# Layer 1's modulation vectors as row sums on VectorE, during layer 0's feed-forward block

## Chip, core and metric

One Trainium2 chip, one of its cores, one launch of the whole program. The metric is the time of the launch on the device in microseconds (us). The trace is that of one profiled execution; the times shown are of separate runs.

## What is computed

A two-layer trunk over 512 latent tokens and 256 context tokens with a model width of 1024. Each layer first makes six modulation vectors of 1024 values per stream (latent: from `c`; context: from `c_ctx`), then runs a mixer and a SwiGLU feed-forward block, each behind a modulated RMS norm. Cut to what matters here:

```python
silu_c, silu_cc = jax.nn.silu(c), jax.nn.silu(c_ctx)
for l in range(DEPTH):                                  # 2 layers
    m  = silu_c  @ ada_w[l] + ada_b[l]                  # (1024) @ (1024, 6144)
    mc = silu_cc @ ada_w[l] + ada_b[l]
    sh_m, sc_m, g_m, sh_f, sc_f, g_f = split(m, 6)
    csh_m, csc_m, cg_m, csh_f, csc_f, cg_f = split(mc, 6)
    h, hc = rms_norm(x) * (1 + sc_m) + sh_m, rms_norm(ctx) * (1 + csc_m) + csh_m
    ...                                                 # layer 0: diff. attention and DeltaNet; layer 1: neighbourhood attention
    x = x + g_m * o
    x = x + g_f * swiglu(rms_norm(x, norm_ffn[l]) * (1 + sc_f) + sh_f)
    if l == 0:                                          # the context is dropped after layer 0
        ctx = ctx + cg_m * oc
        ctx = ctx + cg_f * swiglu(rms_norm(ctx) * (1 + csc_f) + csh_f)
return x
```

In layer 1 the context uses its modulation only for the shift and scale ahead of the mixer (`csh_m`, `csc_m`); its other four vectors are not used.

## The kernel before

Activations lie transposed: eight tiles of 128 model channels by 768 token columns (256 of the context, 512 latent). Every large product is done as three float32r matmuls on high and low parts (`mm3`, L176): the weight tile is loaded into a staging tile `st` by SyncE's DMA queue (SP), its high part `whi` is a copy on ScalarE (L164), its low part `wlo` is a subtraction on VectorE (L165).

Layer 0's feed-forward block (`ffn`) runs in four groups of hidden tiles (6, 5, 6 and 5). An *up step* is one hidden tile: two weight tiles of 128x1024 (gate and up), then for each stretch of tokens two rows of 24 matmuls into PSUM tiles `f`, Silu on ScalarE, the product `sg` on VectorE (L1409), and its parts `mh` (ScalarE, L1410) and `ml` (VectorE, L1411). A *down tile* is one of eight column tiles of the group's down projection: one weight tile, two rows of matmuls (512 latent, 256 context columns), and the update of `x` on VectorE (L1421).

The *entrance* of the block is where the mixer's output projection and the block's norm overlap. The tokens go in thirds (context, then each half of the latent tokens). For each third eight updates `x<-o` (L1332) run on VectorE, squares on ScalarE (L294) and their sums on VectorE or GpSimd (L296). `finish` (L298 on) then makes the mean `ms` (L309), the inverse root (a seed `rs_y` on VectorE, L190, then a chain of small steps on GpSimd, L193 to L202), its broadcast `rb` on TensorE (L313), and for each of eight channel tiles the normed tile `nt` (L316) and its parts `hhi` (ScalarE, L324) and `hlo` (VectorE, L325; the last tile's on GpSimd). The first hidden tile's up step takes the three thirds one by one, as they come.

Layer 1's modulation vectors are made while layer 0's feed-forward block runs. `ada_gen` is a generator with one step for each of 48 tiles of `ada_w` (128x1024, 512 KB): a DMA into the staging tile `ast` (two buffers, SP's queue, L1380) and four matmuls with 32 stationary columns into the PSUM tile `adacc` (L238). After each eighth tile the sums are copied to `adrow` (L243), turned by two transposes (`adtp`, L249) and added to the bias (L252). `ada_step` asks for one step: ahead of each weight split of an up step (two per hidden tile), and ahead of the one split of a down tile. 48 steps thus lie in group 0 (6 hidden tiles, 8 column tiles), group 1 (5 and 8) and five hidden tiles of group 2. A scheduler then sets the order on each engine from the program's dependencies and priorities; engines run their instructions in that order.

```python
for t in range(t0, t0 + ng):
    ws = []
    for z in range(2):
        ada_step()
        ws.append(kx.wsplit(a["wfi"][l, t, z], 1024))
    for s, sl in (segs if t else fine):
        up(mh, ml, ws, sl)
...
for c in range(KT - tail):
    ada_step()
    ws = kx.wsplit(a[f"wfo{gi}"][l, c], 128 * ng)
    for s, sl in segs:
        down(mids, c, ws, s, sl, cnt)
```

Of the kernel before, what the change touches and what calls it, by code (L numbers as in the profile page):

```python
# [15 lines left out]
D = 1024  # L16
# [3 lines left out]
KT = 8  # L20
# [51 lines left out]
def MARK(name):  # L72
    pass
# [51 lines left out]
def build(tc, a, out, dbg=None):  # L125
    nc = tc.nc
    V, G, S, T, DMA = nc.vector, nc.gpsimd, nc.scalar, nc.tensor, nc.sync
    es = ExitStack()
    with es:
# [4 lines left out]
        def ct(name, shape, dt=F32):  # L134
            return cp.tile(shape, dt, name=name, tag=name)
# [10 lines left out]
        def load_const(name, key, shape):  # L146
            t = ct(name, shape)
            DMA.dma_start(out=t, in_=a[key])
            return t

        cvec = load_const("cvec", "cT", [128, KT, 2])
        ada_b = load_const("ada_b", "ada_b", [128, 2, 48])
        nrm = load_const("nrm", "nrm", [128, 2, 2, KT])

        def wstage(src, n):
            st = wp.tile([128, n], F32, name="st", tag="st", bufs=2)
            if src is not None:
                DMA.dma_start(out=st, in_=src)
            return st

        def wsplit(src, n, tiles=None):
            st = wstage(src, n)
            hi, lo = tiles or [wp.tile([128, n], F32R, name="w" + t, tag="w" + t, bufs=3) for t in ("hi", "lo")]
            S.activation(out=hi, in_=st, func=AF.Copy)  # L164
            V.tensor_tensor(out=lo, in0=st, in1=hi.bitcast(F32), op=ALU.subtract)  # L165
            return hi, lo

        nops = []
        dep = mybir.DependencyInfo(mybir.DependencyClass.Sync, mybir.DependencyReason.DATA)

# [14 lines left out]
        def rsqrt(pool, v, n, tag="rs", N=None):  # L185
            N = N or V
            y = pool.tile([128, n], F32, name="rs_y", tag=tag + "y")
            t = pool.tile([128, n], F32, name="rs_t", tag=tag + "t")
            vh = pool.tile([128, n], F32, name="rs_v", tag=tag + "v")
            V.tensor_scalar(  # L190
                out=y.bitcast(I32), in0=v.bitcast(I32), scalar1=1, scalar2=-1, op0=ALU.logical_shift_right, op1=ALU.bitwise_xor
            )
            N.tensor_scalar(out=y, in0=y, scalar1=RS_SEED, scalar2=None, op0=ALU.mult)  # L193
            N.tensor_scalar(out=vh, in0=v, scalar1=-0.5, scalar2=None, op0=ALU.mult)
            for _ in range(3):
                N.tensor_tensor(out=t, in0=y, in1=y, op=ALU.mult)
# [25 lines left out]
        scal = {}  # L222

        def ada_block(*args, **kw):
            for _ in ada_gen(*args, **kw):
                pass

        def ada_gen(l, b, psp, mk, stage=None, gap=1200, kg=KT):
            lab(f"ada{l}{b}")
            sc = ct(f"scal{l}{b}", [128, 2, 16])  # L230
            for hf in range(2):
                row = cp.tile([128, 256], F32, name="adrow", tag="adrow")
                for k in range(KT):
                    st = (stage or wstage)(a["ada_w"][l, b, hf, k], 1024)
                    if k % kg == 0:
                        acc = psp.tile([128, 256], F32, name="adacc", tag=mk)
                    for j in range(4):
                        T.matmul(  # L238
                            out=acc[32 * j:32 * j + 32, :], lhsT=scT[:, k, :], rhs=st[:, 256 * j:256 * j + 256],
                            start=(k % kg == 0), stop=(k % kg == kg - 1), tile_position=(0, 32 * j),  # L240
                        )
                    if k == kg - 1:
                        V.tensor_copy(out=row, in_=acc)  # L243
                    elif k % kg == kg - 1:
                        V.tensor_tensor(out=row, in0=acc, in1=row, op=ALU.add)
                    yield 450, gap
                tp = psp.tile([128, 2, 128], F32, name="adtp", tag=mk)
                for q in range(2):
                    T.transpose(out=tp[:, q, :], in_=row[:, q * 128:q * 128 + 128], identity=ident)  # L249
                for s in range(2):  # L250
                    o = 16 * b + 8 * hf
                    V.tensor_tensor(  # L252
                        out=sc[:, s, 8 * hf:8 * hf + 8].rearrange("p (j q) -> p j q", q=2),
                        in0=tp.rearrange("p q (j u) -> p j q u", u=32)[:, :, :, s],
                        in1=ada_b[:, l, o:o + 8].rearrange("p (j q) -> p j q", q=2), op=ALU.add,
                    )
            names = [("sh_m", "sc_m"), ("g_m", "sh_f"), ("sc_f", "g_f")][b]
            for i, nm in enumerate(names):
                for s in range(2):
                    v = sc[:, s, 8 * i:8 * i + 8]  # L260
                    if nm.startswith("sc"):
                        w = 0 if nm == "sc_m" else 1
                        t = ct(f"gain{l}{w}{s}", [128, KT])
                        V.scalar_tensor_tensor(out=t, in0=v, scalar=1.0, in1=nrm[:, l, w, :], op0=ALU.add, op1=ALU.mult)
                        scal[l, "a_m" if w == 0 else "a_f", s] = t
                    else:
                        scal[l, nm, s] = v
            yield 500, 0

        def new_h(lat_only=False):  # L270
            hi = [hp.tile([128, NT], F32R, name=f"hhi{k}", tag=f"hhi{k}") for k in range(KT)]
            lo = [hp.tile([128, NT], F32R, name=f"hlo{k}", tag=f"hlo{k}") for k in range(KT)]
            return hi, lo

        class Norm:
            def __init__(self, x, l, w, pool, ps, segs):
                self.on_v, self.rs, self.lo_g = NORMS[f"n{l}{w}"]
                self.x, self.pool, self.ps, self.segs = x, pool, ps, segs
                self.av = [scal[l, "a_" + w, s] for s in range(2)]
                self.sv = [scal[l, "sh_" + w, s] for s in range(2)]  # L280
                self.ssq = [None] * len(segs)
                self.h = None

# [49 lines left out]
        kx = types.SimpleNamespace(**env)  # L333
# [9 lines left out]
        hi, lo = new_h()  # L343
# [18 lines left out]
        with tc.tile_pool(name="x0", bufs=1) as x0p:  # L362
# [13 lines left out]
            for j in range(4):  # L376
# [15 lines left out]
                r = rsqrt(x0p, ms, 6)  # L392
                rb = x0p.tile([128, NT], F32, name="rb", tag="rb")
                for i, sl in enumerate((CTX, LAT)):
                    n = sl.stop - sl.start
                    bp = x0v.tile([128, n], F32, name="bp", tag=f"v{4 + i}")
                    for j in range(n // 128):
                        c = sl.start // 128 + j
# [968 lines left out]
def ffn(kx, x, l, nm, next_norm):  # L1367
    tc, nc, a = kx.tc, kx.nc, kx.a
    V, G, S, T, DMA = nc.vector, nc.gpsimd, nc.scalar, nc.tensor, nc.sync
    scal, gs = kx.scal, kx.gs  # L1370
# [3 lines left out]
    hi, lo = nm.h  # L1374

    with tc.tile_pool(name="fp", bufs=2) as fp:
# [4 lines left out]
            return st  # L1381

        def adas():
            for b in range(3):
                yield from kx.ada_gen(1, b, gs, "C", stage=astage, kg=KT)

        ada_it = adas() if l == 0 else iter(())

        def ada_step():
# [260 lines left out]
def layout(inp):  # L1650
    import numpy as np

    g = {k: np.asarray(v) for k, v in inp.items()}
    f = np.ascontiguousarray
    o = {}
# [4 lines left out]
    cv = np.stack([g["c"][0], g["c_ctx"]], axis=-1)  # L1660
    o["cT"] = f(cv.reshape(KT, 128, 2).transpose(1, 0, 2))
    o["ada_w"] = f(g["ada_w"].reshape(2, KT, 128, 3, 2, 1024).transpose(0, 3, 4, 1, 2, 5))
    o["ada0"] = f(g["ada_w"][0, :, 0:2048].reshape(KT, 128, 2, 4, 2, 128).transpose(3, 1, 0, 2, 4, 5).reshape(4, 128, KT, 4, 128))
    o["ada_b"] = f(g["ada_b"].reshape(2, 48, 128).transpose(2, 0, 1))
    nr = np.stack([g["norm_mix"], g["norm_ffn"]], axis=1)
# [10 lines left out]
    w = g["even_w_in"][0]  # L1676
# [16 lines left out]
    w = g["odd_w_in"][0]  # L1693
# [54 lines left out]
```

## Time and profile before

| | |
|---|---|
| three runs | 1989.01, 1991.40, 1993.08 us (median 1991.4) |
| the profiled execution | 1988.47 us, span of the trace 1986.7 us |
| mean granted TensorE clock, share of full speed | 0.979 |
| busy in the span | TensorE 94%, VectorE 51%, ScalarE 37%, GpSimd 13% |
| HBM | 202.39 MB read, 32.99 MB written, mean 118 GB/s |
| DMAs of the 48 weight tiles concerned | 512 KB each, median 3.6 us from issue to landing |

Times in a row of the trace are microseconds from the span's start. A row of the timeline gives start, duration, engine, line, operation, result<-operands, shapes and count; what stands in brackets is the engine's idle time ahead of it and what ended that. The chain of waits is followed back from the end: a row there is a stretch of the span that this work sets. PE is TensorE, DVE VectorE, ACT ScalarE, POOL GpSimd, SP SyncE.

### The profile page before, as it was taken

How to read it: one execution, taken by the hardware profiler on the slowest of the kernel's cores; microseconds unless marked ns; L12 is line 12 of the kernel's file. 1: busy time of each engine (PE TensorE's matmuls, PEld its weight loads, DVE VectorE, ACT ScalarE, POOL GpSimd, SP SyncE). 2: the span in 40 equal slices, each digit the busy share in tenths (PEclk: the TensorE clock that was granted, in tenths of full speed). 3: DMA queues.
4: the chain of work that ended last, by engine and by line, in shares of the span. 5: the costliest groups of instructions: out<-in, count | busy, mean ns of one | idle time of the engine just before them, and what ended most of it. 6: DMA issues, size and time to landing. Idle time of an engine off the chain costs nothing.

```text
span 1986.7 us, 30896 instructions
## 1 busy us (share of the span) xinstructions
PE 1863.4 (94%) x12066; PEld 1629.6 (82%) x12066; DVE 1013.8 (51%) x2340; ACT 743.9 (37%) x1681; POOL 257.1 (13%) x360
## 2 busy tenths in 40 slices
PE   4978999798989999999999999989999989999999
PEld 3867889677868888888888888989999878888887
DVE  6566788776676662232222232456565663434333
ACT  3435454345664342112112112355555443223221
POOL 2132314421210130000000000321101020000000
PEclk8989999899999999999999999999999989999999
DMA  7556644547444623333343121211211213323232
GB/s 292 156 180 205 205 144 146 179 142 210 112 157 132 226 96 115 120 123 109 119 138 125 56 75 52 87 45 63 65 59 45 71 40 106 106 76 116 85 106 95
DMA packets 105074, 237.41 MB, mean 119 GB/s; under 512 B 10880, under 2 KB 48000, under 8 KB 103904
## 3 DMA queue, kind: packets, MB, share of 16 engines
q1 hardware_dynamic: 92400, 207.26, 32.5%
q0 software_dynamic: 4064, 14.38, 2.6%
q10 hardware_dynamic: 8464, 13.79, 2.0%
q8 instruction: 95, 1.56, 0.3%
q14 instruction: 51, 0.42, 0.1%
HBM read 202.39 MB, written 32.99 MB: 118 GB/s over the span
## 4 chain that ended last, share of the span: by engine, by line
PE 75%; DMA 9%; DVE 7%; ACT 4%; issue 3%; POOL 2%; SPq 0%; ACTq 0%; DVEq 0%; POOLq 0%
PE f L176 46%; PE d L176 15%; DMA qkd<-ar 3%; PE o L176 2%; PE adacc L238 2%; PE vp L448 1%; PE sc L1556 1%; PE o L1581 1%; DMA st<-in_ada_w_dram 1%; DVE cv L351 1%; PE m L854 1%; DMA qkvd<-cv 1%; PE S L1150 1%; PE m L1570 1%; PE t L1178 1%
## 5 line engine op out<-in xcount | busy, mean ns | idle before, releaser
L164 ACT ACTIVATE whi<-st 128x1024 fp32r<-128x1024 f32 (+4 forms) x219 | 212.2, 970 | 608.3 <-PE f L176 456.9
L176 PE MATMUL f<-hhi,whi 128*128 128x512 f32 (+1 forms) x1088 | 381.4, 353 | 3.2 <-ACT hhi L324 3.2
L176 PE MATMUL f<-hlo,whi 128*128 128x512 f32 (+1 forms) x1088 | 381.1, 351 | 0.6 <-DVE hlo L325 0.6
L176 PE MATMUL f<-hhi,wlo 128*128 128x512 f32 (+1 forms) x1088 | 380.2, 350 | 0.0
L165 DVE TENSOR_TENSOR wlo<-st,whi 128x1024 fp32r<-128x1024 f32 (+4 forms) x219 | 247.1, 1129 | 257.6 <-ACT whi L164 253.4
L176 PE MATMUL d<-whi,hhi 128*128 128x256 f32 (+1 forms) x800 | 235.2, 296 | 21.2 <-ACT ar L207 13.9
L176 PEld LDWEIGHTS f<-hhi,whi 128*128 128x128 f32 x1088 | 207.1, 191 | 36.1 <-ACT whi L164 5.4
L176 PE MATMUL d<-wlo,hhi 128*128 128x256 f32 (+1 forms) x800 | 232.9, 292 | 1.3 <-DVE wlo L165 1.3
L176 PE MATMUL d<-whi,hlo 128*128 128x256 f32 (+1 forms) x800 | 232.2, 292 | 0.0
L176 PEld LDWEIGHTS f<-hlo,whi 128*128 128x128 f32 x1088 | 207.6, 191 | 28.0 <-DVE hlo L325 1.2
L176 PEld LDWEIGHTS f<-hhi,wlo 128*128 128x128 f32 x1088 | 207.8, 191 | 26.8 <-issue 0.4
L176 PEld LDWEIGHTS d<-whi,hhi 128*128 128x128 f32 x800 | 156.9, 197 | 28.0 <-ACT ar L207 15.1
L176 PE MATMUL f<-mh,whi 128*128 128x512 f32 (+1 forms) x478 | 171.3, 360 | 0.0
L176 PE MATMUL f<-ml,whi 128*128 128x512 f32 (+1 forms) x478 | 170.0, 356 | 0.0
L176 PE MATMUL f<-mh,wlo 128*128 128x512 f32 (+1 forms) x478 | 168.9, 356 | 0.0
L176 PEld LDWEIGHTS d<-wlo,hhi 128*128 128x128 f32 x800 | 157.3, 197 | 2.5 <-DVE wlo L165 1.7
L176 PEld LDWEIGHTS d<-whi,hlo 128*128 128x128 f32 x800 | 156.6, 196 | 1.0
L1409 DVE TENSOR_TENSOR sg<-f,sg 128x512 f32<-128x512 f32 (+1 forms) x68 | 40.1, 589 | 229.5 <-PE f L176 228.8
L1421 DVE SCALAR_TENSOR_TENSOR x<-f,scal,x 128x256 f32<-128x256 f32 (+1 forms) x101 | 64.1, 639 | 169.0 <-PE f L176 168.7
L296 POOL TENSOR_TENSOR ssq<-ssq,sq 128x256 f32<-128x256 f32 x39 | 31.0, 797 | 677.4 <-ACT sq L294 676.2
L176 PE MATMUL d<-hhi,whi 128*128 128x512 f32 (+1 forms) x304 | 107.2, 353 | 5.0 <-ACT cin L207 2.6
L176 PEld LDWEIGHTS f<-mh,whi 128*128 128x128 f32 x478 | 90.2, 189 | 18.5 <-issue 6.2
(373 smaller groups left out, 3416.9 us busy)
## 6 DMA issues: line engine op xcount, KB each, us to landing
st<-in_wfi_dram SPq DMA_DIRECT2D x88, 512.0 KB, 3.5
ast<-in_ada_w_dram SPq DMA_DIRECT2D x48, 512.0 KB, 3.6
st<-in_ada_w_dram SPq DMA_DIRECT2D x32, 512.0 KB, 4.0
st<-in_wfo_dram SPq DMA_DIRECT2D x32, 384.0 KB, 3.0
st<-in_wfo_dram SPq DMA_DIRECT2D x32, 320.0 KB, 2.8
aw<-in_ada_dram SPq DMA_DIRECT2D x8, 1024.0 KB, 12.3
st<-in_w1kv_dram SPq DMA_DIRECT2D x16, 512.0 KB, 3.8
aqT<-qkd SPq DMA_DIRECT2D x48, 128.0 KB, 3.2
```

Of the source, the lines that this page charges most:

```text
L164: S.activation(out=hi, in_=st, func=AF.Copy)
L165: V.tensor_tensor(out=lo, in0=st, in1=hi.bitcast(F32), op=ALU.subtract)
L176: r = T.matmul(out=ps, lhsT=p, rhs=q, start=(c == 0), stop=(c == n - 1))
L238: T.matmul(out=acc[32 * j:32 * j + 32, :], lhsT=scT[:, k, :], rhs=st[:, 256 * j:256 * j + 256], start=(k % kg == 0), stop=(k % kg == kg - ...
L296: (V if k >= self.on_v else G).tensor_tensor(out=self.ssq[i], in0=self.ssq[i], in1=sq, op=ALU.add)
L351: V.scalar_tensor_tensor(out=cv, in0=cin[:, i:i + 772], scalar=convw[:, tix, i:i + 1], in1=cv, op0=ALU.mult, op1=ALU.add)
L448: T.matmul(out=vp[i, s], lhsT=w[:, ws], rhs=h[k][:, sl], start=(k == 0 and q == 0), stop=(k == KT - 1 and q == 2),)
L854: T.matmul(out=ps[:, i, :], lhsT=lhs[:, c, :], rhs=rhs[:, c, :], start=True, stop=True)
L1150: T.matmul(out=ps[:, o:o + w], lhsT=u.q[:, part, :], rhs=kst[:, m, sl], start=(i == 0), stop=(i == 1))
L1178: T.matmul(out=ov, lhsT=PT[:, i, :], rhs=vt[:, u.kts[i], :], start=(i == 0), stop=(i == u.nk - 1))
L1409: V.tensor_tensor(out=sg, in0=pss[1], in1=sg, op=ALU.mult)
L1421: V.scalar_tensor_tensor(out=o, in0=ps, scalar=scal[l, "g_f", s][:, c:c + 1], in1=o, op0=ALU.mult, op1=ALU.add,)
```

## The change

For layer 1 `ada_rows` takes the place of `ada_gen`. The weights are also handed over transposed (`ada_t`: 48 tiles with 128 output values on the partitions and 1024 inputs along the row, 512 KB each), and `cbc` holds `c` and `c_ctx` on all 128 partitions (128x2x1024, 1 MB). At the first `ada_step`, `cbc` is loaded on SP's queue and passed through Silu on ScalarE in one instruction of 2048 columns. Each of the 48 steps loads one tile into `ast` and multiplies it on VectorE by the row of `cbc`; the instruction's accumulator output, the sum along the row, is the column of 128 modulation values. For the first 16 tiles (shift and scale ahead of the mixer) it is done twice, for the latent and the context row, for the other 32 once: 64 row sums. The product itself goes to a tile `junk`, or over `ast`. Three additions of the bias end the three blocks. Gone are the 192 matmuls, the six `adrow` copies, 12 transposes and 12 additions.

Each row sum also carries a dependency on the latest `wlo` subtraction of a weight split; both are on VectorE, so it is an order and no semaphore.

```diff
         def wsplit(src, n, tiles=None):
...
             S.activation(out=hi, in_=st, func=AF.Copy)
-            V.tensor_tensor(out=lo, in0=st, in1=hi.bitcast(F32), op=ALU.subtract)
+            last_lo[:] = [V.tensor_tensor(out=lo, in0=st, in1=hi.bitcast(F32), op=ALU.subtract).ins]
             return hi, lo
 
+        last_lo = []
+        after = mybir.DependencyInfo(mybir.DependencyClass.NoSync, mybir.DependencyReason.DATA)
...
+        def ada_names(l, b, sc, ns):
             names = [("sh_m", "sc_m"), ("g_m", "sh_f"), ("sc_f", "g_f")][b]
             for i, nm in enumerate(names):
-                for s in range(2):
+                for s in range(ns):
...
+        def ada_rows(l, b, ns, stage, cbc, junk):
+            lab(f"ada{l}{b}")
+            sc = ct(f"scal{l}{b}", [128, 2, 16])
+            for j in range(16):
+                st = stage(a["ada_t"][l, 16 * b + j], 1024)
+                for s in range(ns):
+                    r = V.scalar_tensor_tensor(
+                        out=junk if s < ns - 1 else st, in0=st, scalar=1.0, in1=cbc[:, s, :], op0=ALU.mult, op1=ALU.mult,
+                        accum_out=sc[:, s, j:j + 1],
+                    )
+                    tc.add_manual_dep(r.ins, last_lo[0].name, after, reason="pace")
+                yield 0, 0
+            for s in range(ns):
+                V.tensor_tensor(out=sc[:, s, :], in0=sc[:, s, :], in1=ada_b[:, l, 16 * b:16 * b + 16], op=ALU.add)
+            ada_names(l, b, sc, ns)
+            yield 0, 0
...
         def adas():
+            cbc = fp.tile([128, 2, 1024], F32, name="cbc", tag="cbc", bufs=1)
+            DMA.dma_start(out=cbc, in_=a["cbc"])
+            S.activation(out=cbc, in_=cbc, func=AF.Silu)
+            junk = fp.tile([128, 1024], F32, name="junk", tag="junk", bufs=1)
             for b in range(3):
-                yield from kx.ada_gen(1, b, gs, "C", stage=astage, kg=KT)
+                yield from kx.ada_rows(1, b, 1 if b else 2, astage, cbc, junk)
```

What the change moves shows in the order of the instructions. Line numbers behind the edit are larger by 2 to 26: `x<-o` is L1354 in place of L1332, `hlo` L347 for L325, the row sum L281. First VectorE at the entrance, from the context third's last updates to the second third's first, before (`x6`, `x7` are channel tiles, the numbers behind `_` buffers):

```order
L1332 SCALAR_TENSOR_TENSOR x5_7340<-o_7609,scal01_1093,x5_7340 128x256
L1332 SCALAR_TENSOR_TENSOR x6_7341<-o_7620,scal01_1093,x6_7341 128x256
L190 TENSOR_SCALAR rs_y_7501<-ms_7499 128x2
L296 TENSOR_TENSOR ssq1_7563<-ssq1_7563,sq_7617 128x256
L1332 SCALAR_TENSOR_TENSOR x7_7342<-o_7631,scal01_1093,x7_7342 128x256
L296 TENSOR_TENSOR ssq1_7563<-ssq1_7563,sq_7628 128x256
L1332 SCALAR_TENSOR_TENSOR x0_7335<-o_7701,scal01_1093,x0_7335 128x256
```

The same stretch after the change:

```order
L1354 SCALAR_TENSOR_TENSOR x5_7340<-o_7609,scal01_1093,x5_7340 128x256
L281 SCALAR_TENSOR_TENSOR junk_7853,scal10_7854<-ast_7855,cbc_7850 128x1024
L1354 SCALAR_TENSOR_TENSOR x6_7341<-o_7620,scal01_1093,x6_7341 128x256
L192 TENSOR_SCALAR rs_y_7501<-ms_7499 128x2
L281 SCALAR_TENSOR_TENSOR ast_7855,scal10_7854<-ast_7855,cbc_7850 128x1024
L1354 SCALAR_TENSOR_TENSOR x7_7342<-o_7631,scal01_1093,x7_7342 128x256
L281 SCALAR_TENSOR_TENSOR junk_7853,scal10_7854<-ast_7865,cbc_7850 128x1024
L1354 SCALAR_TENSOR_TENSOR x0_7335<-o_7701,scal01_1093,x0_7335 128x256
```

Three row sums stand among the updates, the first ahead of `x6` and so ahead of the seed `rs_y` of the context third.

Then VectorE further on, around the context third's first `hlo`, before:

```order
L316 SCALAR_TENSOR_TENSOR nt_7534<-x3_7338,gain011_5901,rb_7519 128x256
L165 TENSOR_TENSOR wlo_8053<-st_8050,whi_8052 128x1024
L296 TENSOR_TENSOR ssq2_7709<-ssq2_7709,sq_7763 128x256
L190 TENSOR_SCALAR rs_y_7647<-ms_7645 128x2
L325 SCALAR_TENSOR_TENSOR hlo0_7488<-nt_7522,scal01_1093,hhi0_7480 128x256
L325 SCALAR_TENSOR_TENSOR hlo1_7489<-nt_7526,scal01_1093,hhi1_7481 128x256
```

and after the change:

```order
L338 SCALAR_TENSOR_TENSOR nt_7534<-x3_7338,gain011_5901,rb_7519 128x256
L165 TENSOR_TENSOR wlo_8049<-st_8046,whi_8048 128x1024
L281 SCALAR_TENSOR_TENSOR ast_8042,scal10_7854<-ast_8042,cbc_7850 128x1024
L281 SCALAR_TENSOR_TENSOR junk_7853,scal10_7854<-ast_8052,cbc_7850 128x1024
L318 TENSOR_TENSOR ssq1_7563<-ssq1_7563,sq_7639 128x256
L347 SCALAR_TENSOR_TENSOR hlo0_7488<-nt_7522,scal01_1093,hhi0_7480 128x256
...
L347 SCALAR_TENSOR_TENSOR hlo3_7491<-nt_7534,scal01_1093,hhi3_7483 128x256
L281 SCALAR_TENSOR_TENSOR ast_8052,scal10_7854<-ast_8052,cbc_7850 128x1024
L318 TENSOR_TENSOR ssq2_7709<-ssq2_7709,sq_7763 128x256
L338 SCALAR_TENSOR_TENSOR nt_7538<-x4_7339,gain011_5901,rb_7519 128x256
L338 SCALAR_TENSOR_TENSOR nt_7542<-x5_7340,gain011_5901,rb_7519 128x256
L338 SCALAR_TENSOR_TENSOR nt_7546<-x6_7341,gain011_5901,rb_7519 128x256
L192 TENSOR_SCALAR rs_y_7647<-ms_7645 128x2
```

Seven row sums now stand ahead of the first `hlo` and an eighth ahead of `nt` of the fifth channel tile; the seed `rs_y` of the second third, which stood ahead of the first `hlo`, comes behind the third `nt` of that second half.

Last SP's DMA queue from the load of `x7` on, before:

```order
L1310 DMA x7_7342<-x1d7_106 128x768
L1380 DMA ast_7852<-in_ada_w_dram 128x1024
L1380 DMA ast_7865<-in_ada_w_dram 128x1024
L158 DMA st_8062<-in_wfi_dram 128x1024
L158 DMA st_8186<-in_wfi_dram 128x1024
L1380 DMA ast_8044<-in_ada_w_dram 128x1024
L1380 DMA ast_8056<-in_ada_w_dram 128x1024
```

and after the change:

```order
L1332 DMA x7_7342<-x1d7_106 128x768
L1407 DMA cbc_7850<-in_cbc_dram 128x2048
L1402 DMA ast_7855<-in_ada_t_dram 128x1024
L1402 DMA ast_7865<-in_ada_t_dram 128x1024
L1402 DMA ast_8042<-in_ada_t_dram 128x1024
L1402 DMA ast_8052<-in_ada_t_dram 128x1024
L158 DMA st_8056<-in_wfi_dram 128x1024
```

The 1 MB of `cbc` stands where the first two weight tiles stood, and the next two, which need the buffers that the first row sums free, stand ahead of the weight tile `st` of hidden tile 1.

## Rows read from the trace of the kernel before

**Rows 1.** Page: busy time by engine, share of the span, instructions.

```profile
PE 1863.4 (94%) x12066; PEld 1629.6 (82%) x12066; DVE 1013.8 (51%) x2340; ACT 743.9 (37%) x1681; POOL 257.1 (13%) x360
```

**Rows 2.** Chain of waits, one up step of group 0: start, us, engine, work.

```profile
763.23 1.00 PE adacc L238 x16
764.23 16.86 PE f L176 x96
781.09 0.22 PE adtp L249 x2
```

**Rows 3.** Timeline of DVE, up steps with (1101) and without (1186) the burst.

```profile
1101.33 0.69 DVE L1409 TENSOR_TENSOR sg<-f,sg 128x512 f32<-128x512 f32 x1 [3.42 <-PE f L176]
...
1108.28 0.42 DVE L1409 TENSOR_TENSOR sg<-f,sg 128x256 f32<-128x256 f32 x1 [4.46 <-PE f L176]
...
1186.13 0.69 DVE L1409 TENSOR_TENSOR sg<-f,sg 128x512 f32<-128x512 f32 x1 [3.37 <-PE f L176]
1186.98 1.23 DVE L165 TENSOR_TENSOR wlo<-st,whi 128x1024 fp32r<-128x1024 f32 x1 [0.15 <-ACT whi L164]
...
1191.89 0.42 DVE L1409 TENSOR_TENSOR sg<-f,sg 128x256 f32<-128x256 f32 x1 [3.08 <-PE f L176]
```

**Rows 4.** Timeline of DVE, down tiles of group 0 (831) and group 2 (1131).

```profile
831.87 0.75 DVE L1421 SCALAR_TENSOR_TENSOR x<-f,scal,x 128x512 f32<-128x512 f32 x1 [3.62 <-PE f L176]
...
838.90 0.75 DVE L1421 SCALAR_TENSOR_TENSOR x<-f,scal,x 128x512 f32<-128x512 f32 x1 [3.62 <-PE f L176]
...
1131.85 0.75 DVE L1421 SCALAR_TENSOR_TENSOR x<-f,scal,x 128x512 f32<-128x512 f32 x1 [3.62 <-PE f L176]
...
1138.11 0.75 DVE L1421 SCALAR_TENSOR_TENSOR x<-f,scal,x 128x512 f32<-128x512 f32 x1 [3.62 <-PE f L176]
```

**Rows 5.** Groups of DVE by line and shape: busy us, mean ns; idle before.

```profile
L351 DVE SCALAR_TENSOR_TENSOR cv<-cin,convw,cv 128x772 f32<-128x772 f32 x48 | 49.0, 1022 | 0.5
L1164 DVE SCALAR_TENSOR_TENSOR e<-e,acf 128x768 f32<-128x768 f32 x16 | 18.1, 1130 | 0.1
L1421 DVE SCALAR_TENSOR_TENSOR x<-f,scal,x 128x256 f32<-128x256 f32 x42 | 20.2, 482 | 24.7 <-PE f L176 24.6
```

**Rows 6.** Timeline of ACT: an accumulator read, a split, a table load.

```profile
660.86 0.19 ACT L987 ACTIVATION_READ_ACCUMULATOR u<-oacc 128x1 f32 x1
...
662.80 1.06 ACT L164 ACTIVATE whi<-st 128x1024 fp32r<-128x1024 f32 x1 [0.45 <-PE d L176]
...
712.64 1.28 ACT L1408 ACT_TABLE_LOAD   x1
```

**Rows 7.** Timeline of DVE, the entrance.

```profile
690.72 2.04 DVE L1332 SCALAR_TENSOR_TENSOR x<-o,scal,x 128x256 f32<-128x256 f32 x5
694.08 0.21 DVE L190 TENSOR_SCALAR rs_y<-ms 128x2 int32<-128x2 int32 x1 [1.31 <-ACT ms L309]
...
703.99 0.16 DVE L190 TENSOR_SCALAR rs_y<-ms 128x2 int32<-128x2 int32 x1
704.06 1.66 DVE L325 SCALAR_TENSOR_TENSOR hlo<-nt,scal,hhi 128x256 fp32r<-128x256 f32 x4
...
710.23 1.66 DVE L316 SCALAR_TENSOR_TENSOR nt<-x,gain,rb 128x256 f32<-128x256 f32 x4 [1.08 <-PE rb L313]
```

**Rows 8.** Busy us by stretch: PE, PEld, DVE, ACT, POOL; clock; DMA share; GB/s.

```profile
680.00:690.00 10.00, 10.00 (x85) 9.98 (x84) 5.63 (x13) 3.55 (x9) 2.97 (x4) 1.00 0.78 252
690.00:695.00 5.00, 4.92 (x41) 4.71 (x40) 3.68 (x11) 2.85 (x8) 3.54 (x7) 1.00 0.02 10
...
705.00:710.00 5.00, 5.00 (x28) 5.00 (x28) 4.15 (x11) 2.22 (x5) 4.01 (x12) 0.58 0.22 88
```

**Rows 9.** Chain of waits through the entrance.

```profile
711.89 0.09 DVE rs_y L190
...
716.45 0.71 PE rb L313 x4
717.16 1.00 PE adacc L238 x16
```

More of the change, by code (lines that the diff above doesn't have):

```diff
@@ L256, in ada_gen @@
                     )
+            ada_names(l, b, sc, 2)
+            yield 500, 0
+        def ada_names(l, b, sc, ns):
             names = [("sh_m", "sc_m"), ("g_m", "sh_f"), ("sc_f", "g_f")][b]
             for i, nm in enumerate(names):
-                for s in range(2):
+                for s in range(ns):
                     v = sc[:, s, 8 * i:8 * i + 8]
@@ L267, in ada_gen @@
                         scal[l, nm, s] = v
-            yield 500, 0
+        def ada_rows(l, b, ns, stage, cbc, junk):
[14 more added lines that the diff above has]
+            yield 0, 0
         def new_h(lat_only=False):
@@ L278, in __init__ @@
                 self.x, self.pool, self.ps, self.segs = x, pool, ps, segs
-                self.av = [scal[l, "a_" + w, s] for s in range(2)]
-                self.sv = [scal[l, "sh_" + w, s] for s in range(2)]
+                self.av = [scal.get((l, "a_" + w, s)) for s in range(2)]
+                self.sv = [scal.get((l, "sh_" + w, s)) for s in range(2)]
                 self.ssq = [None] * len(segs)
@@ L1662, in layout @@
     o["ada_w"] = f(g["ada_w"].reshape(2, KT, 128, 3, 2, 1024).transpose(0, 3, 4, 1, 2, 5))
+    o["ada_t"] = f(g["ada_w"].reshape(2, D, 48, 128).transpose(0, 2, 3, 1))
+    o["cbc"] = f(np.broadcast_to(np.stack([g["c"][0], g["c_ctx"]])[None], (128, 2, D)))
     o["ada0"] = f(g["ada_w"][0, :, 0:2048].reshape(KT, 128, 2, 4, 2, 128).transpose(3, 1, 0, 2, 4, 5).reshape(4, 128, KT, 4, 128))
```

## The prediction

> **What bounds the kernel now.** I read the page first, for the busiest engine. TensorE is busy 94% of the span and VectorE 51% [rows 1], so what leaves TensorE's stream can shorten the span and what VectorE takes on can hide, stage by stage. The chain of waits then tells who sets the time where the modulation tiles are made. In layer 0's feed-forward block one up step is a burst of `adacc`, then 96 matmuls of `f` back to back for 16.86 us, then the next burst [rows 2]: nothing but TensorE stands in the chain there. The timeline of VectorE tells what a step takes with and without the burst [rows 3, 4]. Last I read the entrance, where the change puts its first row sums [rows 7 to 9]. There VectorE is the engine that others wait for: between 690 and 704 it runs from one instruction into the next with one gap of 1.31 us [rows 7], and TensorE stands ready.
>
> The profiled execution took 1988.5 us, 2.9 less than the median of 1991.4. The sum below is a difference; I apply it to the median.
>
> **What goes.** From one `sg` of 512 columns to the next of 256 it takes 1108.28 - 1101.33 = 6.95 us with a burst between and 1191.89 - 1186.13 = 5.76 without [rows 3]: 1.19 an up step. Down tiles follow each other by 838.90 - 831.87 = 7.03 with their half burst and 1138.11 - 1131.85 = 6.26 without [rows 4]: 0.77 each. Of the 16 up steps with bursts two lie in the entrance and are counted there. The others give 14 x 1.19 = 16.7, the 16 down tiles 16 x 0.77 = 12.3, and the six pairs of transposes 0.22 each [rows 2], 1.3. Sum: 30.3 us. The lower end takes the chain's rows alone, 1.00 for a burst of two tiles [rows 2] and half of it for one: 14 + 8 + 1.3 = 23.3. I take 30.3, since the pitch holds also what a burst costs around itself.
>
> **The price of a row sum.** No VectorE instruction in the trace writes an accumulator. The nearest is the same operation with two float32 sources in SBUF: 1.02 us for 772 columns (`cv`) and 1.13 for 768 (`e`) [rows 5]. From 256 to 512 columns it grows by 0.75 - 0.48 = 0.27 [rows 4, 5], so 1024 would be 1.3, by `e` 1.4. ScalarE pays 0.19 for its accumulator read [rows 6]; if VectorE does too, 1.6 is the upper end. The lower is 1.2, as successive instructions overlap a little (four `nt` take 1.66, not 4 x 0.48 [rows 5, 7]). I take 1.3, from `cv`, the commonest.
>
> The rule that speaks against this comes by itself: the Trainium skill, "Vector Engine (DVE) Microarchitecture Reference", § 7 "Points that are easy to get wrong", states that this instruction with two non-bf16 SBUF sources halves throughput, since no read port is left for the accumulator's readback. The rows of `cv` and `e` do not show a halving, but neither of them accumulates; by the rule the sum would be that of rival 1.
>
> **Where row sums hide.** In an up step VectorE needs two `wlo` of 1.23 and twice 0.69 + 0.42 for `sg` and `ml` (`ml` counted like `sg`): 4.7 of the 16.86 us [rows 2, 3]. Four row sums add 5.2, two add 2.6. Ahead of each `sg` VectorE idles 3.1 to 4.5 us [rows 3], and of an `x` update 3.6 [rows 4]; a pair of row sums, 2.6, fits. If one is in the way, `sg` is late by at most that pair, and TensorE has the other row of matmuls to do meanwhile. VectorE would bound a step only from (16.86 - 4.7) / 4 = 3.0 us a row sum. The order behind the latest `wlo` names an instruction of the same engine and costs no wait. The three bias additions replace twelve; the six `adrow` copies go too. I cost all this at nothing. The DMAs are as many and as large; SP's queue alternates `st` and `ast` as before, and an `ast` buffer is free after its row sums rather than after four matmuls, inside the same step.
>
> **What the entrance pays.** Here nothing covers. I follow VectorE in four steps.
>
> (1) The first row sum stands ahead of `x6`, the last of the five updates that begin at 690.72 [rows 7], so VectorE comes to it at about 692.3. It needs `cbc` through Silu. `cbc` is 1 MB behind `x7` in SP's queue, where two `ast` of 512 KB stood, and thus lands when those did: the DMA moves 252 GB/s up to 690 and 10 after it [rows 8], so at about 690.5. Then ScalarE needs a table, 1.28, and 2048 columns at twice 1.06 [rows 6], 3.4 together with some squares between: ready at about 694.3, a wait of 2.0. `x6` and the seed `rs_y` of the context third stand behind it.
>
> (2) Seven row sums, 7 x 1.3 = 9.1, stand ahead of the first `hlo`. The gap of 1.31 is filled. So it starts at 704.06 + 2.0 + 9.1 - 1.3 = 713.9 in place of 704.06 [rows 7], and TensorE, which waits for it, 9.8 later.
>
> (3) The seed `rs_y` of the second third was at 703.99, just ahead of that `hlo` [rows 7]. Now it comes behind four `hlo` (1.66), the eighth row sum (1.3) and three `nt` (1.25): 713.9 + 1.66 + 1.3 + 1.25, less its own 0.16, is 718.0. From seed to broadcast GpSimd's chain takes 716.45 - 711.89 = 4.6, and the broadcast 0.71 [rows 9], so the first `nt` is at 723.3 against 710.23 [rows 7]: 13 us late. The cover is gone: before, this chain ran beside the matmuls of the context third.
>
> (4) The last third's seed stands behind this `nt` as before, and its chain sets the time as before [rows 9]: 13 us late too. On it stood a burst of `adacc`, 1.00 at 717.16 [rows 9], which goes. Loss: 12 us. TensorE can win back little, as it was busy for all of 705 to 710 [rows 8].
>
> The ends of the loss: without the wait for `cbc` and with 1.2 a row sum it is 12 - 2.0 - 0.8 = 9, and with some slack in the last third 6; with 1.6 it is 12 + 8 x 0.3 = 14.4, and if TensorE, which came out of its half-idle stretch at a granted clock of 0.58 for 5 us [rows 8], loses those 2.1 us once more, 16.5.
>
> **The sum.** -30.3 + 12 = -18.3, so 1991.4 - 18.3 = **1973**. Its own range: 1991.4 - 30.3 + 6 = 1967 to 1991.4 - 23.3 + 16.5 = 1985.
>
> **Rivals.**
>
> 1. *The row sum runs at half rate*, as a second pass for the accumulator. 2 x (1.3 - 0.1 of fixed cost) is about 2.35. In steady steps it still hides, being under 3.0. In the entrance VectorE stays the bound through the last `sg` of hidden tile 1, ahead of which 14 row sums stand (8 to the fifth channel tile, 6 more): 14 x 1.05 = 15 more, a loss of 27 and a net of -3.6: 1988. For it: nothing that accumulates on VectorE was seen. Against it: `cv` at 1.02 for 772 columns [rows 5], against 0.75 for 512 with a source in PSUM [rows 4], shows no slow second SBUF source.
>
> 2. *Slower: VectorE becomes the bound of the entrance so far that the loss exceeds the 30 gained.* One mechanism: the 14 row sums ahead of that last `sg`. It decides from 1.3 + 18.3 / 14 = 2.6 us each. At 3.0 the loss is 12 + 14 x 1.7 = 36, the net +5.5: 1997. Group 0's steps would then be bound by VectorE as well. For it speaks only that the price is not seen; against it the same rows of `cv` and `e`.
>
> 3. *The change does not give TensorE's time back*: the bursts filled time in which the `f` stream would have waited for its weights. Then only the loss is left, +12: 2003. Against it: 6.95 against 5.76, and 7.03 against 6.26, are steps of the same kernel with and without the burst [rows 3, 4].
>
> 4. *The entrance costs only 5*, because the matmuls of the last third cover more than I allow: 1991.4 - 25.3 = 1966. For it: TensorE has two hidden tiles' work there; against it: the chain, which runs through `rs_y` and `rb` [rows 9].
>
> **How the numbers follow.** A measurement of this kernel tells about 0.2%, 4.0 us, from no change. My forecast gets 0.76, rival 1 0.13, rival 2 0.04, rival 3 0.03, rival 4 0.04. The forecast and rival 4 are faster, 0.80; rival 1 lies at -3.6, next to the bound, and I split it 0.07 faster and 0.06 same; rivals 2 and 3 are slower, 0.07. So faster 0.87, same 0.06, slower 0.07. The range goes from 1965, just under rival 4, to 1988, which takes in rival 1; left out are rivals 2 and 3 and the tails of rival 1.
>
> **What would show it.** In the profile after: row sums of about 1.3 us on VectorE, and no wait of `f` matmuls in groups 0 to 2; up steps of group 0 at the pitch of those of group 2 without bursts, 5.76 from `sg` to `sg`, and down tiles at 6.26; `cbc`'s Silu ending near 694; the first `hlo` near 714, the second third's first `nt` near 723, the third's 13 after its place of before. The prediction is wrong if a row sum takes 2.3 or more, if `f` waits for `sg` or `wlo` in the steady steps, or if the first down tile of group 0 is later or earlier than the steady gain and a loss of 12 give.

## The result, and the profile after

The changed kernel takes 1971.3 us (median of 5 runs, 1963.3 to 1977.0), the kernel before 1989.0 (median of 5, 1987.4 to 1993.1): a ratio of 0.9905, 95% interval 0.9877 to 0.9934, so 19 us faster. Forecast were 1973 us and 18.3 us. The profiled execution took 1970.7 us, 17.8 less than that of before.

The page's first part, of the changed kernel: TensorE is 31 us less busy, VectorE 72 us more [rows 1].

```profile
PE 1832.6 (93%) x11670; PEld 1625.2 (83%) x11670; DVE 1086.1 (55%) x2453; ACT 745.8 (38%) x1682; POOL 260.5 (13%) x360
```

The row sums, all instructions of line 281 (the durations are minimum, median and maximum in ns, then the first and last start):

```profile
L281 DVE SCALAR_TENSOR_TENSOR ast<-ast,cbc x48: 1212/1218/1739, 697.1 to 1069.4; 128x1024 f32<-128x1024 f32 x48
L281 DVE DVE_READ_ACCUMULATOR ast<-ast,cbc x48: 77/83/89, 698.2 to 1070.5; 128x1 f32 x48
L281 DVE SCALAR_TENSOR_TENSOR junk<-ast,cbc x16: 1218/1219/1731, 695.3 to 827.1; 128x1024 f32<-128x1024 f32 x16
```

A row sum of 1024 columns takes 1.22 us, and its accumulator read, an instruction of its own, 0.08. The read overlaps the end of the product, so the two cost 1.2 and not 1.3. The maximum of 1.74 is the first thing to note: three row sums took 1.5 to 1.7, and all three lie in the entrance.

VectorE's timeline of the changed kernel through the entrance, to be held against [rows 7]:

```profile
689.37 0.48 DVE L1354 SCALAR_TENSOR_TENSOR x<-o,scal,x 128x256 f32<-128x256 f32 x1 [0.72 <-DMA x<-x1d]
...
695.33 1.23 DVE L281 SCALAR_TENSOR_TENSOR junk<-ast,cbc 128x1024 f32<-128x1024 f32 x1 [1.63 <-ACT cbc L1408]
...
696.88 0.31 DVE L192 TENSOR_SCALAR rs_y<-ms 128x2 int32<-128x2 int32 x1
...
702.10 1.22 DVE L281 SCALAR_TENSOR_TENSOR ast<-ast,cbc 128x1024 f32<-128x1024 f32 x1
...
703.64 1.22 DVE L165 TENSOR_TENSOR wlo<-st,whi 128x1024 fp32r<-128x1024 f32 x1
...
705.17 1.22 DVE L281 SCALAR_TENSOR_TENSOR junk<-ast,cbc 128x1024 f32<-128x1024 f32 x1
...
708.68 1.66 DVE L338 SCALAR_TENSOR_TENSOR nt<-x,gain,rb 128x256 f32<-128x256 f32 x4 [1.16 <-PE rb L335]
...
711.82 1.74 DVE L281 SCALAR_TENSOR_TENSOR ast<-ast,cbc 128x1024 f32<-128x1024 f32 x1
...
713.49 1.73 DVE L281 SCALAR_TENSOR_TENSOR junk<-ast,cbc 128x1024 f32<-128x1024 f32 x1
...
715.49 1.66 DVE L347 SCALAR_TENSOR_TENSOR hlo<-nt,scal,hhi 128x256 fp32r<-128x256 f32 x4
...
719.73 0.16 DVE L192 TENSOR_SCALAR rs_y<-ms 128x2 int32<-128x2 int32 x1
...
725.81 1.66 DVE L338 SCALAR_TENSOR_TENSOR nt<-x,gain,rb 128x256 f32<-128x256 f32 x4 [0.21 <-PE rb L335]
...
733.92 1.66 DVE L338 SCALAR_TENSOR_TENSOR nt<-x,gain,rb 128x256 f32<-128x256 f32 x4 [1.71 <-PE rb L335]
```

The traces do not reach the entrance at the same time. The update that waits for its tile from DRAM, the last row ahead of any difference, starts at 688.54 in the trace of before:

```profile
688.54 0.48 DVE L1332 SCALAR_TENSOR_TENSOR x<-o,scal,x 128x256 f32<-128x256 f32 x1 [3.06 <-DMA x<-x1d]
```

So 0.83 us of every lag in this trace is older than the change; in other kernels' traces it is up to 7. (In the two kernels that load `cbc` earlier, that load stands ahead of this row, so for them the row is not ahead of every difference.) Below, "lag" is the start of an `sg` or `nt`, less its start in the trace of before, less this offset. The wait for Silu is 1.63 (forecast 2.0). The first `hlo` lags by 715.49 - 704.06 - 0.83 = 10.6 (9.8), the second third's first `nt` by 14.8 (13), the last third's by 733.92 - 717.20 - 0.83 = 15.9 (13).

From the broadcast of the last third on, TensorE has its work in hand. The chain of waits of the changed kernel from there to the last up step is one row:

```profile
733.88 506.25 PE f L178 x2940
```

So from here on the difference between the kernels is what TensorE has to do. Three rows of `sg` of 512 columns show the balance: those of hidden tiles 1 and 2, and the last of the block. First after, then before:

```profile
758.97 0.69 DVE L1435 TENSOR_TENSOR sg<-f,sg 128x512 f32<-128x512 f32 x1 [0.56 <-PE f L178]
...
775.70 0.69 DVE L1435 TENSOR_TENSOR sg<-f,sg 128x512 f32<-128x512 f32 x1 [1.01 <-PE f L178]
...
1234.30 0.68 DVE L1435 TENSOR_TENSOR sg<-f,sg 128x512 f32<-128x512 f32 x1
```

```profile
745.48 0.69 DVE L1409 TENSOR_TENSOR sg<-f,sg 128x512 f32<-128x512 f32 x1 [3.42 <-PE f L176]
...
763.34 0.69 DVE L1409 TENSOR_TENSOR sg<-f,sg 128x512 f32<-128x512 f32 x1 [3.42 <-PE f L176]
...
1253.26 0.68 DVE L1409 TENSOR_TENSOR sg<-f,sg 128x512 f32<-128x512 f32 x1
```

The lag is 758.97 - 745.48 - 0.83 = 12.7 at hidden tile 1, 12.36 - 0.83 = 11.5 at hidden tile 2, and -19.8 at the last. The forecast's gain counts the bursts from hidden tile 2 on, 14 of them, and the first of these lies between the first two rows. Divided as the forecast divides, it is **12.7 lost at the entrance (forecast 12), 32.4 gained behind it (forecast 30.3)**. The table below takes the row of hidden tile 2, the first up step in which the late starts have row sums; there the same balance reads 11.5 and 31.3. A down tile of group 0 shows where the row sum lies, in what was VectorE's idle time; the pitch of `x` updates is 844.38 - 838.12 = 6.26, that of a tile without a burst [rows 4]:

```profile
838.12 0.75 DVE L1447 SCALAR_TENSOR_TENSOR x<-f,scal,x 128x512 f32<-128x512 f32 x1 [3.03 <-PE f L178]
838.82 0.96 DVE L165 TENSOR_TENSOR wlo<-st,whi 128x768 fp32r<-128x768 f32 x1
839.70 1.22 DVE L281 SCALAR_TENSOR_TENSOR ast<-ast,cbc 128x1024 f32<-128x1024 f32 x1
...
844.38 0.75 DVE L1447 SCALAR_TENSOR_TENSOR x<-f,scal,x 128x512 f32<-128x512 f32 x1 [3.06 <-PE f L178]
```

### The profile page after: what moved, and what is told of

The parts are those of the page before. It is cut to its first block, busy times and chain, and to the rows that moved or that the text cites. A ratio compares the mean times of both kernels' runs of the same rounds, so it can differ in the third digit from the quotient of the medians.

```text
span 1968.7 us, 30208 instructions
## 1 busy us (share of the span) xinstructions
PE 1832.6 (93%) x11670; PEld 1625.2 (83%) x11670; DVE 1086.1 (55%) x2453; ACT 745.8 (38%) x1682; POOL 260.5 (13%) x360
## 4 chain that ended last, share of the span: by engine, by line
PE 75%; DVE 8%; DMA 8%; ACT 3%; issue 3%; POOL 2%; SPq 0%; ACTq 0%; POOLq 0%; DVEq 0%
PE f L178 46%; PE d L178 16%; PE o L178 2%; DMA qkd<-ar 1%; PE vp L470 1%; PE sc L1582 1%; PE o L1607 1%; PE S L1172 1%; DMA MB<-md 1%; PE m L876 1%; DMA md<-dec 1%; PE t L1200 1%; DVE cv L373 1%; PE m L1596 1%; DMA st<-in_ada_w_dram 1%
## 5 line engine op out<-in xcount | busy, mean ns | idle before, releaser
L178 PEld LDWEIGHTS d<-whi,hhi 128*128 128x128 f32 x800 | 156.5, 196 | 28.7 <-ACT ar L209 17.8
L178 PE MATMUL d<-hhi,wlo 128*128 128x512 f32 (+1 forms) x304 | 105.3, 347 | 0.0
```

The lines of the kernel that those rows point to most:

```text
L178: r = T.matmul(out=ps, lhsT=p, rhs=q, start=(c == 0), stop=(c == n - 1))
```

## The experiments

Eight kernels were run. The table has each one's ratio to the kernel before, run in turns with it (the kernels were run in three sets, so compare ratios rather than medians), and from its profiled execution the offset ahead of the entrance, the lag at hidden tile 2 and the gain from there to the last up step.

| kernel | median, us | ratio, 95% interval | offset | lag at tile 2 | from there on |
|---|---|---|---|---|---|
| the change | 1971.3 | 0.9905 [0.9877, 0.9934] | 0.8 | 11.5 | -31.3 |
| no modulation work | 1957.3 | 0.9827 [0.9803, 0.9851] | 2.5 | -3.7 | -31.0 |
| late start | 1961.4 | 0.9840 [0.9819, 0.9861] | 4.5 | -1.1 | -31.1 |
| late start, `cbc` earlier | 1962.6 | 0.9852 [0.9819, 0.9886] | 2.7 | -1.5 | -31.1 |
| `cbc` earlier | 1972.3 | 0.9901 [0.9880, 0.9922] | 3.5 | 9.0 | -31.0 |
| late start, `cbc` behind | 1952.8 | 0.9800 [0.9775, 0.9825] | 1.1 | -4.5 | -31.3 |
| reductions at the entrance | 1968.3 (one run) | | 3.2 | 8.0 | -31.0 |
| no order behind `wlo` | 1992.3 | 0.9992 [0.9978, 1.0007] | 1.2 | 23.2 | -21.2 |
| late start, row sums twice | 1964.1 | 0.9841 [0.9810, 0.9872] | 7.0 | 0.2 | -31.2 |

**1. No modulation work**: the floor.

```diff
-                yield from kx.ada_rows(1, b, 1 if b else 2, astage, cbc, junk)
+                yield from kx.ada_none(1, b, 1 if b else 2)
...
+            for s in range(ns):
+                V.tensor_copy(out=sc[:, s, :], in_=ada_b[:, l, 16 * b:16 * b + 16])
```

> Layer 1's modulation work is left out altogether: no weight tiles, no cbc, no row sums; the vectors are the bias alone. It is the floor under every version. If the row sums of the steady steps are hidden, as I hold, the steady part is the changed kernel's: -31.0 us there (from the shift of +12.4 at hidden tile 2's first sg to -18.6 behind the last tile), and the two bursts of the entrance go as well, 2 x 1.2, so 33.4 below the kernel before: about 1956. If row sums cost something in the steady steps, say 0.2 us each for the 56 behind the entrance, the floor lies 11 lower, at 1945.

Measured 0.9827, some 34 us below before. From hidden tile 2 on it gains 31.0, as the change does: the steady row sums, their loads and their place in VectorE's order cost nothing that shows. Its lag of -3.7 at hidden tile 2 is about what three bursts held there. They are in the chain of waits of the kernel before, the first of them at 717.16 [rows 9] and the second in two pieces:

```profile
725.43 0.99 PE adacc L238 x12
...
729.24 0.56 PE adacc L238 x4
...
745.37 1.00 PE adacc L238 x16
```

1.00 + 0.99 + 0.56 + 1.00 = 3.55. Against this floor the change loses 11.5 + 3.7 = 15.2 us at its entrance.

**2. Late start**: the first four steps are skipped and done later.

```diff
                 for z in range(2):
-                    ada_step()
+                    if t >= 2:
+                        ada_step()
```

> The changed kernel with its first row sums four steps later, at hidden tile 2; cbc's load and Silu stay where they were, in the entrance. My theory: the loss at the entrance (12.4 us by the shift of sg at hidden tile 2) is the row sums' own time on VectorE and what stands behind them, so it goes, all but some 0 to 2 us for the 3.2 us of ScalarE that Silu takes: 1956 to 1958. Rival: the loss comes with cbc, by its 1 MB in SP's queue and by Silu ahead of the squares: 1966 to 1969, little better than the change.

0.9840. The lag goes from 11.5 to -1.1, so the loss is that of the eight row sums at the entrance and of what stands behind them, as I held; the rival falls for most of it. The edit also takes their four loads out of the entrance; but in the change's chain of waits no load stands between 691 and the broadcast at 733, so the loads are not what it waited for. But 2.6 remain against the floor, more than the 0 to 2 I allowed Silu.

**3 and 4. `cbc` some places earlier**, with the late start and without it.

```diff
     kx.np = xes.enter_context(tc.tile_pool(name="np", bufs=1, side="right"))
+    kx.cbc = kx.np.tile([128, 2, 1024], F32, name="cbc", tag="cbc", bufs=1)
+    kx.nc.sync.dma_start(out=kx.cbc, in_=kx.a["cbc"])
+    kx.nc.scalar.activation(out=kx.cbc, in_=kx.cbc, func=AF.Silu)
```

> As the late start, and cbc's load and Silu some places earlier, when the block's pools are opened, among the context third's squares. My theory: within 2 us of the late start, 1956 to 1958, since no row sum is near and Silu is as long at either place. The rival (cbc costs): it depends on where the load and Silu stand, 1960 or less here against 1966 to 1969 for the late start alone.

> The changed kernel with cbc's load and Silu some places earlier, and nothing else by the edit; the order then has three row sums in place of one ahead of the context third's seed. My theory: the wait of 1.6 us for Silu goes, and 2 x 1.2 us come ahead of that seed, so no gain that can be told: 1969 to 1973. Rival (cbc's arrival sets the loss): most of the 12 us goes, 1960.

0.9852 and 0.9901: neither can be told from its partner (0.9840, 0.9905). The wait for `cbc` is not what makes the loss. By the traces the second one's lag is 2.5 smaller, more than I expected of it; the runs don't show that. The offset may account for it: in this kernel `cbc`'s load is issued at 678.9, ahead of that of the `x` tile whose update gives the offset (687.6). Without subtracting offsets the two lags are 12.55 and 12.36.

**5. Late start with `cbc` behind the entrance**: Silu is ordered on ScalarE behind hidden tile 1's `mh`.

```diff
-            S.activation(out=mh[:, sl], in_=sg, func=AF.Copy)
+            kx.last_mh = [S.activation(out=mh[:, sl], in_=sg, func=AF.Copy).ins]
...
-            S.activation(out=cbc, in_=cbc, func=AF.Silu)
+            r = S.activation(out=cbc, in_=cbc, func=AF.Silu)
+            tc.add_manual_dep(r.ins, kx.last_mh[0].name, kx.after, reason="pace")
```

> The late start, with cbc's Silu ordered on ScalarE behind the mh copy of hidden tile 1, so that neither its table load nor its 1.9 us stand among the entrance's squares; cbc's load stays where it was. The late start lies some 4 us above the floor without modulation work (1961.4 against 1957.3). My theory: about 2.6 of these are Silu's 3.2 us of ScalarE at the entrance (sg of hidden tile 2, less the entrance's own later start in that trace: -1.1 for the late start, -3.7 for the floor), so 1957 to 1959, 34 below before. Rival: the rest is the load's 1 MB in SP's queue, or row sums that do not hide: 1961 to 1962 as for the late start.

0.9800, **the fastest of all**, 40 us below before; its interval overlaps that of the floor, and its lag at hidden tile 2 is no worse than the floor's (-4.5 against -3.7; why it is better by 0.8 was not followed). Its interval also touches that of the late start, so the step from one to the other rests on the traces, -1.1 against -4.5: it was Silu's place on ScalarE that cost the late start its rest. Two rows of VectorE and one of ScalarE, first of the late start, show how the context third's seed waits:

```profile
696.92 1.92 ACT L1408 ACTIVATE cbc<-cbc 128x2048 f32<-128x2048 f32 x1
```

```profile
699.62 0.42 DVE L192 TENSOR_SCALAR rs_y<-ms 128x2 int32<-128x2 int32 x1 [2.17 <-ACT ms L331]
...
708.09 1.37 DVE L165 TENSOR_TENSOR wlo<-st,whi 128x1024 fp32r<-128x1024 f32 x1 [1.53 <-ACT whi L164]
709.38 1.64 DVE L338 SCALAR_TENSOR_TENSOR nt<-x,gain,rb 128x256 f32<-128x256 f32 x4
```

and then of this kernel:

```profile
744.47 1.90 ACT L1408 ACTIVATE cbc<-cbc 128x2048 f32<-128x2048 f32 x1
```

```profile
695.20 0.20 DVE L192 TENSOR_SCALAR rs_y<-ms 128x2 int32<-128x2 int32 x1 [0.18 <-ACT ms L331]
...
702.06 1.66 DVE L338 SCALAR_TENSOR_TENSOR nt<-x,gain,rb 128x256 f32<-128x256 f32 x4
```

Less their offsets (4.45 and 1.12) the seed comes at 695.2 and 694.1, and the first `nt` at 704.9 and 700.9. Silu puts off the squares. More of their sums then fall among the root's steps on GpSimd (from the seed to the last step 8.1 us in place of 6.1), and the first `nt` stands behind a `wlo` that waits for ScalarE.

**6. Reductions in place of the first eight row sums**, one SBUF source in place of two (the product with `cbc` is left out of them).

```diff
+                    if b == 0 and j < 4:
+                        r = V.tensor_reduce(out=sc[:, s, j:j + 1], in_=st, axis=AX.X, op=ALU.add)
+                    else:
...
```

> The changed kernel, but for the first four tiles the row sum is a reduction of the weight tile alone, one SBUF source in place of two and without cbc (these sums leave out the product); it needs about as long on VectorE. The eight of them stand ahead of the first hlo. Theory A (only VectorE's own time counts): wait for Silu gone, -1.6, one sum more ahead of hlo, +1.2: sg of hidden tile 2 some 11 us late, as in the change. Theory B (a VectorE instruction with two SBUF sources holds up GpSimd's steps, which in the change's entrance took 1.1 to 1.3 us in place of 0.2 wherever a row sum or a wlo ran, and is itself held up, 1.7 in place of 1.2): GpSimd's steps beside reductions take 0.2 to 0.4, the context third's broadcast comes 6 to 7 us behind its seed in place of 10.5, and sg of hidden tile 2 is 8 to 9 us late.

This tells apart VectorE's own time from what it does to its neighbour. GpSimd's timeline of the change first, steps of the context third's root chain that lie beside the row sums at 702.10 and 705.17 above, and between them beside a `wlo` at 703.64:

```profile
702.12 1.25 POOL L198 TENSOR_TENSOR rs_t<-rs_y 128x2 f32<-128x2 f32 x1
703.45 0.19 POOL L199 TENSOR_TENSOR rs_t<-rs_t,rs_v 128x2 f32<-128x2 f32 x1
703.73 1.20 POOL L203 TENSOR_SCALAR rs_t<-rs_t 128x2 f32<-128x2 f32 x1
...
705.29 1.15 POOL L198 TENSOR_TENSOR rs_t<-rs_y 128x2 f32<-128x2 f32 x1
...
707.17 0.19 POOL L204 TENSOR_TENSOR rs_y<-rs_y,rs_t 128x2 f32<-128x2 f32 x1
```

Then VectorE and GpSimd of this kernel, the same chain beside two reductions:

```profile
699.75 0.16 DVE L192 TENSOR_SCALAR rs_y<-ms 128x2 int32<-128x2 int32 x1
699.82 2.34 DVE L282 TENSOR_REDUCE scal<-ast 128x1 f32<-128x1024 f32 x2
```

```profile
700.89 0.19 POOL L198 TENSOR_TENSOR rs_t<-rs_y 128x2 f32<-128x2 f32 x1
701.16 0.20 POOL L199 TENSOR_TENSOR rs_t<-rs_t,rs_v 128x2 f32<-128x2 f32 x1
...
704.10 0.20 POOL L204 TENSOR_TENSOR rs_y<-rs_y,rs_t 128x2 f32<-128x2 f32 x1
```

A step on 128x2 values takes 0.2, but 1.15 to 1.25, to the end of the VectorE instruction, where that is a row sum or a `wlo`; beside a reduction of the same 1.2 us it stays at 0.2. From the seed to the chain's last step it takes 704.30 - 699.75 = 4.6 here and 707.36 - 696.88 = 10.5 in the change. The lag is 8.0 in place of 11.5. Theory B said 8 to 9 and holds: about 3.5 of the loss is the two engines holding each other up. That is not GpSimd's chain alone, since the reductions also ran without the 1.3 us that three row sums of the change took beyond 1.22. The waiting time before the first sum is about as long in both (1.6 for `cbc`, 1.5 here for the first `ast`), so it doesn't blur the comparison. The size rests on one profiled execution; its time, 1968.3, lies among those of the change.

The trace of before already had this, one step of the same chain beside a `wlo`:

```profile
697.72 1.79 DVE L165 TENSOR_TENSOR wlo<-st,whi 128x1024 fp32r<-128x1024 f32 x1
```

```profile
698.39 1.17 POOL L197 TENSOR_TENSOR rs_t<-rs_t,rs_v 128x2 f32<-128x2 f32 x1
```

The Trainium skill, "SBUF — State Buffer", § "Who interferes with whom", states that a VectorE instruction with two SBUF inputs contends with a GpSimd instruction that reads SBUF, and that a reduction never does. These rows agree.

**7. No order behind `wlo`.**

```diff
-                    tc.add_manual_dep(r.ins, last_lo[0].name, after, reason="pace")
+                    pass
```

> The changed kernel without the order behind the latest wlo. The scheduler then puts 27 row sums ahead of hidden tile 1's last products where the change has 12, ten weight tiles ast one behind another in SP's queue ahead of the weights of hidden tile 2. If row sums at the entrance cost their time: 15 x 1.2 = 18 more there, less what TensorE wins back: 1980 to 1990. Rival (the order behind wlo is inert, the row sums hide wherever they stand): 1971 as the change.

0.9992: **the whole gain is gone**. At hidden tile 2 the lag is 23.2, 12 more than in the change (18 less what TensorE wins back had been expected). What I had not expected follows: from there on it gains 21 and not 31. VectorE's timeline of hidden tile 2 shows it:

```profile
774.37 1.22 DVE L281 SCALAR_TENSOR_TENSOR ast<-ast,cbc 128x1024 f32<-128x1024 f32 x1 [0.71 <-DMA ast<-in_ada_t_dram]
...
783.97 1.23 DVE L281 SCALAR_TENSOR_TENSOR ast<-ast,cbc 128x1024 f32<-128x1024 f32 x1 [0.48 <-DMA ast<-in_ada_t_dram]
...
786.55 1.23 DVE L281 SCALAR_TENSOR_TENSOR ast<-ast,cbc 128x1024 f32<-128x1024 f32 x1 [1.35 <-DMA ast<-in_ada_t_dram]
787.70 0.08 DVE L281 DVE_READ_ACCUMULATOR ast<-ast,cbc 128x1 f32 x1
787.70 0.69 DVE L1435 TENSOR_TENSOR sg<-f,sg 128x512 f32<-128x512 f32 x1
```

`sg` starts the moment the row sum ahead of it ends, and that row sum has waited for its tile. Over the whole kernel the row sums waited like this 28 times, 28.5 us in all; in the change it was once, for 0.2:

```profile
  DMA ast<-in_ada_t_dram: 28.5, 28
```

With two `ast` buffers a tile takes a load of some 4 us and a row sum of 1.2 after one another, and the scheduler has lined up more of them in VectorE's order than the loads can feed. The next `sg` of 512 columns is 19.1 us later, and 16.66 in the change. The order behind `wlo` is what spreads the row sums at the rate of the weight tiles, and in the change no matmul waits behind it.

**8. Late start, each row sum done twice.**

```diff
-                    r = V.scalar_tensor_tensor(
+                    for o in (junk, junk if s < ns - 1 else st):
+                        r = V.scalar_tensor_tensor(
...
```

> The late start with every row sum done twice, 128 in place of 64, to see how far the cover of the steady steps reaches. VectorE's time in an up step is then 4.7 + 8 x 1.22 = 14.5 of 16.7 us at most, so it hides; in a down tile of group 0, with two tokens' rows of a tile, it is 0.95 + 0.75 + 0.48 + 4 x 1.22 = 7.1 against a pitch of 6.26, so VectorE bounds it and 8 tiles cost 0.8 each. My theory: 6 to 8 above the late start, 1967 to 1970. Rival (the cover is thinner than the busy times say, the order between sg, wlo and row sums matters): 64 x 1.22 = 78 in the worst case, 1990 and more.

0.9841 against 0.9840: 64 more row sums, 64 x 1.22 = 78 us by their length, cost nothing that shows. The intervals are 6 and 4 us wide either way, so the ratios alone could hide the 6 to 8 I expected; the traces decide, with -31.2 from hidden tile 2 on against -31.1. Where I had VectorE as the bound, in group 0's down tiles, it does fill up, 26.26 of 28 us (busy us of PE, PEld, DVE, ACT and POOL, granted clock, DMA share and GB/s of that stretch):

```profile
830.00:858.00 28.00, 28.00 (x159) 24.60 (x159) 26.26 (x45) 3.62 (x5) 0.00 (x0) 1.00 0.47 155
```

but TensorE is busy for all 28. `x` updates then come late by some tenths per tile (846.10 - 839.47 = 6.63 and not 6.26), which the `f` tiles' slack takes up before single row sums follow. My reckoning of 0.8 a tile took a busy sum over the pitch for a loss; it is one only once the slack is used up.

## Why the prediction was right

**The steady gain** came out by its own step, the pitches with and without a burst [rows 3, 4]: from hidden tile 1's `sg` on it is 32.4 where 30.3 was forecast, and from hidden tile 2's on it is 31.0 to 31.3 in the change and seven of the eight other kernels. Where the 2 us more lie was not followed. The lower end by the chain's rows alone, 23.3, was not needed.

**The price of a row sum** (1.3) was 1.22 to 1.23 with the read hidden in it, but for the three that GpSimd's sums held up. The step from `cv` to 1024 columns held; the accumulator costs 0.08 and not 0.19. The Trainium skill's rule on halved throughput of this instruction, in "Vector Engine (DVE) Microarchitecture Reference", § 7, is not what is seen here: two float32 SBUF sources and an accumulator, at 1.22 us for 1024 columns against 1.02 for 772 without one [rows 5].

**The cover in the steady steps** (nothing lost) is shown by the floor and by the doubled row sums, and has more room than 1.2 us a row. The bias additions that replace twelve are four and not three, as the first block has one for each stream; that changes nothing here.

**The loss at the entrance** (12, measured 12.7) was right by errors that offset each other, which is luck in the number. The mechanism of steps (1) to (3) is shown: wait for Silu, seven row sums ahead of `hlo`, the second seed moved behind it, and with the row sums gone the loss goes. Silu itself came as forecast: it ended at 695.3, less the offset 694.5 (694.3). But the terms on the way were too small: 10.6, 14.8 and 15.9 where 9.8, 13 and 13 were forecast. Steps (2) to (4) counted row sums on VectorE alone and took GpSimd's chain as before. They left out that the two engines hold each other up, some 3.5 us in the end: the first `nt` waits 1.16 for its broadcast, and the seven row sums took 9.4 us from each start to the next instruction's, where at 1.15 each (786.55 to 787.70 in run 7) they would have been 8.1.

The other error is in step (4). From the last third's `nt` to hidden tile 2 the lag falls from 15.9 to 11.5, by 4.4. TensorE is without a wait on this stretch in both kernels, so the rows of the chain divide it: 3.55 are the three bursts shown with run 1. The forecast took off the first here and has the third in the gain; the second, 1.55, was to be counted in the entrance and was not. What is left, 0.8, is `f` work (42.5 us of it on this stretch before, 41.7 after), matmuls that TensorE had done earlier; so "TensorE can win back little" held.

**The rivals.** Half rate and the slower side fall with the 1.22 us. (Rival 1's price was worked out too low: doubled but for 0.1 of fixed cost, 1.3 becomes 2.5, not 2.35, and its time would have been about 1990.) That the bursts gave no time back falls with the 31. The cheap entrance, 5, falls with the 12.7. But run 7 shows a slower side that was not among them: had the order behind `wlo` not been there, the gain would have been zero, by waits of row sums for their own tiles and not by their length.

## What to carry to other kernels

Work that goes from a full engine to a half-idle one is worth the time it leaves behind only where the other is idle: split the sum by stage, and begin the moved work behind a stage in which the receiving engine is the one waited for (here worth 40 us in place of 19, with Silu moved too). Give such filler an order that ties it to the steady consumption of something else, so that it can't queue up ahead of the products and wait for its own loads there. And when VectorE takes two SBUF sources, look at what GpSimd does beside it.

## What the runs showed of the hardware that was not expected

A GpSimd step on 128x2 values, 0.2 us long, took 1.15 to 1.25 in the rows above beside a VectorE instruction with two SBUF sources (row sum, `wlo`), and 0.2 beside a reduction. It goes the other way as well: row sums and `wlo` of 1.22 took 1.64 to 1.74 where GpSimd added sums of 128x256 beside them (710.25 to 715.15 in the change). One of these sums:

```profile
711.59 0.88 POOL L318 TENSOR_TENSOR ssq<-ssq,sq 128x256 f32<-128x256 f32 x1 [0.78 <-ACT sq L316]
```

The accumulator read shows as an instruction of 0.08 us that begins where the next one does.
